# Seven-product block multiplication for seven of 22 up-projection pairs, three feed-forward blocks and edge copies on ScalarE, in a two-layer encoder step

## Chip, cores and metric

The kernel runs on one core of one Trainium2 chip. The metric is the device time of one execution in microseconds (us). TensorE (PE) does the matrix products, its weight loads are listed apart (PEld); VectorE (DVE), ScalarE (ACT) and GpSimd (POOL) do the element-wise work; SyncE (SP) issues the DMA transfers.

## The reference, cut to what matters

One inference step of a two-layer encoder for 544 columns of tokens (512 prompt, 32 sample), model width 1024, feed-forward width 2816, all in float32. The part that the change touches is the feed-forward of each layer:

```python
up = x @ lp['ffn_w_up']                                   # (544 x 1024) @ (1024 x 5632)
upc, ffn_conv_new = causal_dwconv(up, ffn_conv_prev, lp['ffn_conv_w'], lp['ffn_conv_b'])   # width 3
g_ff, val = upc[..., :D_FF], upc[..., D_FF:]
f = (jax.nn.gelu(g_ff) * val) @ lp['ffn_w_down']          # (544 x 2816) @ (2816 x 1024)
x = layer_norm(ALPHA * x + f, lp['ln2_g'], lp['ln2_b'])
```

`ffn_conv_new`, the last two rows of `up` of either group, is an output. Before the feed-forward stands the mixer (three head groups, an output projection and a layer norm).

## The kernel before, in words

**Layout.** Activations are kept transposed: a page is 128 features by 544 token columns, eight pages make the model width. Each float32 operand of a large product is split into a high part (a fp32r copy, on ACT) and a low part (source minus high, on DVE): `split` (L77). One k-tile of a product is three matmuls (`mm3`, L87: high x high on L88, high x low on L89, low x high on L90), each 128x128 weights by 272 columns, since a PSUM bank is filled for one half (`hv`) of the columns at a time.

**Feed-forward** (`ffn`, L1019). The 5632 up-projected features are 44 tiles of 128: 22 pairs, a gate tile (s = 0) and a value tile (s = 1). The work goes in two blocks (`NB`, L26) of 11 pairs. In a block, for each tile: `up_w` (L1008) loads 512 KB of weights through one of two raw buffers (`wr`) and splits them into one of five `wh` and one of five `wl` buffers; `mms` (L221) makes 8 k-tiles x 3 matmuls for each half; `ev` (L1031) evacuates: ACT copies the bank to `xp` (L1040) and makes the first convolution tap `ac` from the same bank (L1041). After the second half POOL copies the edge columns, the state in and the new state out (L1043 to L1045), DVE adds the other two taps (L1046, L1048), ACT applies the gelu to a gate tile (L1050), DVE multiplies the value tile with it (L1053), and the product is split into `fh`, `fl` (L1057). Then the block's down-projection runs over its 11 `fh`, `fl` pages: `proj` (L941) after the first block, `proj_ln` (L948) after the second. Both take the output tiles m = 0, 1 together (k-tile by k-tile in turn), then one by one; DVE adds each bank to the page `xT` (L1083, L1093).

**Start of the feed-forward.** While the last output-projection tiles are made, `proj_ln` prepares the weights of the first five up tiles (`pre_up`, L1011). The layer norm writes the pages XH, XL in the order m = 0..7: m = 0..3 before the last evacuations, m = 4..7 after them (L979, L985). `staged` (L1014) makes the first three up tiles together over the k-tiles m = 0..7 and then two tiles one by one; the second half's norm hangs as a hook behind the third k-tile. For the next eight tiles a `settle` (L935) finishes one page `xT` each (L1069).

**What sets the order.** Each engine runs its instructions in an order that is fixed when the program is built: of those that are ready, the one that stands first in the program. So a later piece of work can go ahead of an earlier one that waits, but only where the build foresaw the wait. PSUM has five banks for these products, eight `kb` pages hold `xp` and `ac`, and 28 `pg` and 12 `pt` pages hold the rest. The cache and state loads of the mixer have three raw pages of their own (`cr`).

Of the kernel before, what the change touches and what calls it, by code (L numbers as in the profile page):

```python
# [13 lines left out]
DEPTH = 2  # L14
# [8 lines left out]
PG = 552  # L23
D_FF = 2816
NI = 22
NB = 2  # L26
BI = NI // NB
# [18 lines left out]
def trunk_kernel(ctx: ExitStack, tc: tile.TileContext, i, o, k):  # L46
# [4 lines left out]
    BUFS = dict(pg=28, pt=12, kb=8, pp=6, cr=3, wr=2, wh=5, wl=5)  # L51

    def page(name, dt=F32, tag="pg"):
        return pool.tile([128, PG], dt, tag=tag, name=name, bufs=BUFS[tag])

# [31 lines left out]
    def mm3(ps, lh, ll, rh, rl, start, stop):  # L87
        nc.tensor.matmul(ps, lh, rh, start=start, stop=False)  # L88
        nc.tensor.matmul(ps, lh, rl, start=False, stop=False)  # L89
        lastmm[0] = nc.tensor.matmul(ps, ll, rh, start=False, stop=stop)  # L90

    gate = []
    def load_w(src, kk, cols, name):
        wr = pool.tile([128, kk, cols], F32, tag="wr", name=name + "r", bufs=BUFS["wr"])
        nc.sync.dma_start(out=wr, in_=src)
        return wr

# [135 lines left out]
    KX = [(XH[m], XL[m]) for m in range(8)]  # L233

# [474 lines left out]
    def cache_page(l, n):  # L709
        r = page("cr", tag="cr")  # L710
        nc.sync.dma_start(out=r[:, 0:512], in_=i["ck"][l, n])
        return r[:, 0:512].rearrange("p (t c) -> p t c", t=2)

    def sample_scores(l, ukT, csT):
# [3 lines left out]
        def keys(j):  # L718
            cT = []
            for c in range(2):  # L720
                raw = page("ckT", tag="cr")
# [4 lines left out]
            raw = page("krr", tag="cr")  # L726
# [54 lines left out]
    def sample_out(l, sp, csn):  # L781
# [30 lines left out]
        uvr = [page(f"uvs{c}", tag="cr") for c in range(2)]  # L812
# [201 lines left out]
    def staged(ws, hv, hook):  # L1014
        yield from enumerate(mms(ws[0:3], KX, hv, hook))
        for j in range(3, len(ws)):
            yield j, mms([ws[j]], KX, hv)[0]

    def ffn(l, va, vf, xT, first, hook, rest, pre):  # L1019
        fo = const([128, 176], F32, "fo")  # L1020
        fov = fo.rearrange("p (s j r) -> p s j r", s=2, j=2)

# [3 lines left out]
        for bl in range(NB):  # L1026
            fts = []
            tiles = [(BI * bl + j, s) for j in range(BI) for s in range(2)]
            xp, ac = {}, {}

            def ev(tl, hv, ps):  # L1031
                i_, s = tl
                r = NI * s + i_
                if hv == 0:
                    tag = "pg" if bl == 0 and tiles.index(tl) in (3, 4) else "kb"
                    xp[tl] = page("xp", tag=tag)
                    ac[tl] = page("ac", tag=tag)
                    nc.gpsimd.memset(xp[tl][:, 0:2], 0.0)  # L1038
                x, a = xp[tl], ac[tl]
                act(x[:, 2 + HW * hv:2 + HW * hv + HW], ps)  # L1040
                act(a[:, HV[hv]], ps, AF.Identity, scale=vfc(F_W + 88, r), bias=vfc(F_B, r))  # L1041
                if hv == 1:
# [3 lines left out]
                    stt(a[:, 0:W], x[:, 0:W], vfc(F_W, r), a[:, 0:W], ALU.mult, ALU.add)  # L1046
                    nc.vector.tensor_copy(out=x[:, 512:513], in_=fov[:, 0, 0, r:r + 1])
                    stt(a[:, 0:W], x[:, 1:1 + W], vfc(F_W + 44, r), a[:, 0:W], ALU.mult, ALU.add)  # L1048
                    if s == 0:
                        act(a[:, 0:W], a[:, 0:W], AF.Gelu_apprx_tanh)  # L1050
                    else:
                        g = ac.pop((i_, 0))
                        tt(a[:, 0:W], a[:, 0:W], g[:, 0:W], ALU.mult)  # L1053
                        j = i_ - BI * bl
                        tag = "pt" if (j < 6) == (bl == 0) and (bl == 0 or j >= 5) else "pg"
                        fh, fl = page("fh", F32R, tag), page("fl", F32R, tag)
                        split(fh[:, 0:W], fl[:, 0:W], a[:, 0:W])  # L1057
                        fts.append((fh, fl))
                        ac.pop(tl)
                    xp.pop(tl)  # L1060

            done = 0
            if bl == 0:
                done = len(first)
                for hv in range(2):
                    for j, ps in staged(first, hv, hook if hv == 0 else None):
                        ev(tiles[j], hv, ps)
            for tl in tiles[done:]:
                if rest:  # L1069
                    rest.pop(0)()  # L1070
                w = up_w(l, *tl)
                for hv in range(2):
                    ev(tl, hv, mms([w], KX, hv)[0])
            wd = i["wdn"][l, bl]

            def wsrc(m):
                return wd[m]

            if bl < NB - 1:
# [6 lines left out]
                proj(wsrc, fts, ev2, "wd", 6)  # L1086
            else:
# [6 lines left out]
                nxt = proj_ln(wsrc, fts, ln, "wd", 6, 2, pre, mid)  # L1094
# [26 lines left out]
def _layout(a):  # L1121
# [23 lines left out]
    d["wup"] = units(a["ffn_w_up"], 8)  # L1145
    w = a["ffn_w_down"].reshape(DEPTH, NB, BI, 128, 8, 128)
    d["wdn"] = w.transpose(0, 1, 4, 3, 2, 5).reshape(DEPTH, NB, 8, 128, BI * 128)
# [84 lines left out]
```

## Time and profile before

| what | value |
|---|---|
| median of 3 runs (lowest to highest) | 1288.82 us (1288.14 to 1291.58) |
| the profiled execution: its time | 1291.58 us |
| the profiled execution: its span | 1289.8 us, 24483 instructions |
| mean granted TensorE clock | 0.992 |

The profile is that of the slowest of the three executions. Busy time is per engine; a chain view follows the work that ended last, a wait view says which engine stood idle until what. Matmuls are pipelined, so the duration of one (some 288 ns) is longer than the step from one to the next. Times in the timeline are microseconds from the start of the span.

### The profile page before, as it was taken

To read this page: it belongs to the slowest core of one execution; us is meant where nothing else is said; L and a number is where in the kernel's file an instruction comes from. 1 tells how busy PE (TensorE), PEld (TensorE's weight loads), DVE (VectorE), ACT (ScalarE), POOL (GpSimd) and SP (SyncE) were. 2 spreads that over 40 slices of the span, in tenths; PEclk is the share of its full clock that TensorE was granted. 3 is DMA by queue.
4 is the path that set the end of the run, shared out by engine and by line. 5 is a ranking of instruction groups with operands and counts; after the bars stand their busy time and mean duration, and the time that the engine had idled before them with its cause. 6 is when DMAs were issued, how large, how long until landed. Compare 5 with 4: busy or idle time off the path is not lost.

```text
span 1289.8 us, 24483 instructions
## 1 busy us (share of the span) xinstructions
PE 1266.2 (98%) x9682; PEld 1224.4 (95%) x9682; DVE 835.4 (65%) x1695; ACT 674.4 (52%) x1357; POOL 140.7 (11%) x486
## 2 busy tenths in 40 slices
PE   8999999999999999999999999999999999999995
PEld 8999869899999999999999997899999999999995
DVE  5766866986653355654886868688765435556466
ACT  6575754485542255542475767547655314555332
POOL 2510000021210012210000100000221001121000
PEclk9999989999999999999999999999999999999998
DMA  8333322232213322223344432331322233222222
GB/s 271 116 111 117 107 85 92 66 101 96 74 57 100 117 97 83 81 71 101 93 138 141 120 98 72 101 110 52 100 82 71 72 104 108 90 83 78 61 79 70
DMA packets 51475, 124.63 MB, mean 97 GB/s; under 512 B 7832, under 2 KB 15512, under 8 KB 51360
## 3 DMA queue, kind: packets, MB, share of 16 engines
q1 hardware_dynamic: 51360, 123.06, 30.2%
q8 instruction: 76, 1.25, 0.4%
q14 instruction: 39, 0.32, 0.1%
HBM read 112.61 MB, written 5.97 MB: 92 GB/s over the span
## 4 chain that ended last, share of the span: by engine, by line
PE 91%; DVE 5%; DMA 2%; ACT 1%; issue 0%; DVEq 0%; ACTq 0%; SPq 0%
PE mm L89 25%; PE mm L88 25%; PE mm L90 25%; PE ov L239 2%; DVE xT L69 1%; PE pT L129 1%; PE ol L239 1%; DVE xT L66 1%; PE s L88 1%; PE s L89 1%; PE kv L384 1%; PE kv L383 1%; PE kv L385 1%; PE s L90 1%; DVE lnq L66 1%; DVE wupl L66 1%
## 5 line engine op out<-in xcount | busy, mean ns | idle before, releaser
L88 PE MATMUL mm<-xh,wuph 128*128 128x272 f32 x1408 | 404.0, 288 | 4.0 <-ACT xh L63 4.0
L89 PE MATMUL mm<-xl,wuph 128*128 128x272 f32 x1408 | 406.2, 289 | 0.1
L90 PE MATMUL mm<-xh,wupl 128*128 128x272 f32 x1408 | 405.7, 288 | 0.0
L88 PEld LDWEIGHTS mm<-xh,wuph 128*128 128x128 f32 x1408 | 264.3, 188 | 4.9 <-ACT xh L63 4.9
L89 PEld LDWEIGHTS mm<-xl,wuph 128*128 128x128 f32 x1408 | 265.1, 188 | 0.6 <-DVE xl L69 0.5
L90 PEld LDWEIGHTS mm<-xh,wupl 128*128 128x128 f32 x1408 | 264.7, 188 | 0.1
L66 DVE TENSOR_TENSOR wupl<-wupr,wuph 128x1024 fp32r<-128x1024 f32 (+1 forms) x94 | 108.8, 1157 | 107.4 <-ACT wuph L63 107.1
L69 DVE SCALAR_TENSOR_TENSOR ac<-xp,vf,ac 128x544 f32<-128x544 f32 x176 | 137.6, 784 | 30.3 <-POOL xp L1038 24.2
L1043 POOL COPY fo<-xp 128x2 f32<-128x2 f32 x88 | 73.1, 831 | 558.6 <-ACT xp L63 558.6
L63 ACT ACTIVATE wuph<-wupr 128x1024 fp32r<-128x1024 f32 (+1 forms) x94 | 94.3, 1005 | 65.9 <-PE mm L89 60.4
L63 ACT ACTIVATE xp<-mm 128x272 f32<-128x272 f32 x176 | 68.9, 391 | 106.2 <-PE mm L90 106.2
L63 ACT ACTIVATE ac<-mm,vf 128x272 f32<-128x272 f32 x176 | 101.3, 575 | 0.0
L63 ACT ACTIVATE fh<-ac 128x544 fp32r<-128x544 f32 x44 | 29.1, 661 | 59.2 <-DVE ac L66 59.2
L69 DVE SCALAR_TENSOR_TENSOR xT<-xT,mm 128x272 f32<-128x272 f32 x48 | 20.6, 438 | 52.1 <-PE mm L90 51.9
L66 DVE TENSOR_TENSOR fl<-ac,fh 128x544 fp32r<-128x544 f32 x44 | 31.9, 726 | 31.7 <-ACT fh L63 31.5
L582 DVE TENSOR_REDUCE sma<-s 128x1 f32<-128x128 f32 (+1 forms) x64 | 29.9, 486 | 17.3 <-PE s L90 16.7
L1038 POOL MEMSET xp<- 128x2 f32 x88 | 8.4, 97 | 286.6 <-PE gs L239 159.3
L63 ACT ACTIVATE ac<-ac 128x544 f32<-128x544 f32 x44 | 29.0, 660 | 20.2 <-DVE ac L69 20.1
L63 ACT ACTIVATE p<-s,sma 128x128 f32<-128x128 f32 (+1 forms) x64 | 33.4, 528 | 11.1 <-DVE sma L582 9.8
L63 ACT ACTIVATE lnt<-xT 128x272 f32<-128x272 f32 x56 | 22.6, 427 | 27.3 <-DVE xT L66 27.0
L66 DVE TENSOR_TENSOR ac<-ac 128x544 f32<-128x544 f32 x44 | 31.9, 725 | 1.4
L66 DVE TENSOR_TENSOR xT<-xT,mm 128x272 f32<-128x272 f32 x48 | 20.1, 439 | 18.7 <-PE mm L90 18.7
(490 smaller groups left out, 3461.3 us busy)
## 6 DMA issues: line engine op xcount, KB each, us to landing
wupr<-in_wup_dram SPq DMA_DIRECT2D x88, 512.0 KB
xT<-in_x_dram SPq DMA_DIRECT2D x16, 136.0 KB
xT<-in_x_dram SPq DMA_DIRECT2D x8, 272.0 KB
xd<-xT SPq DMA_DIRECT2D x8, 272.0 KB
xT<-xd SPq DMA_DIRECT2D x8, 272.0 KB
out_dram<-xT SPq DMA_DIRECT2D x16, 136.0 KB
ckT<-in_ckT_dram SPq DMA_DIRECT2D x8, 256.0 KB
cr<-in_ck_dram SPq DMA_DIRECT2D x8, 256.0 KB
```

The lines of the kernel that those rows point to most:

```text
L63: return nc.scalar.activation(out=out, in_=in_, func=func, **kw)
L66: return (e or nc.vector).tensor_tensor(out=out, in0=a, in1=b, op=op)
L69: return nc.vector.scalar_tensor_tensor(out=out, in0=a, scalar=s, in1=b, op0=op0, op1=op1)
L88: nc.tensor.matmul(ps, lh, rh, start=start, stop=False)
L89: nc.tensor.matmul(ps, lh, rl, start=False, stop=False)
L90: lastmm[0] = nc.tensor.matmul(ps, ll, rh, start=False, stop=stop)
L129: nc.tensor.transpose(out, in_, ident[0:p, 0:p])
L239: nc.tensor.matmul(ps, a, b, start=start, stop=stop)
L383: nc.tensor.matmul(b[0:n, 0:288], XH[j][:, cs], wh[:, ci, :], start=j == 0, stop=False)
L384: nc.tensor.matmul(b[0:n, 0:288], XL[j][:, cs], wh[:, ci, :], start=False, stop=False)
L582: nc.vector.tensor_reduce(out=sm[:, 0:1], in_=b[:, 0:n], axis=AX.X, op=ALU.max, negate=True)
L1043: nc.gpsimd.tensor_copy(out=fov[:, 0, :, r], in_=x[:, 512:514])
```

## The change

- Seven pairs of each layer (`SPL`: 8, 10, ..., 20) are made by a block multiplication with seven products instead of eight. The 2x2 blocks are: gate tile and value tile, the two halves of the model width, the two halves of the columns. `forms` makes the seven weight blocks (A11, A12, A22 and four sums) from the two raw weight tiles and splits them: three splits of 128x1024 and one of 128x512, and four DVE sums of 128x512. `mixed_x` makes four sums of the token halves for each pair of pages, once per layer, and splits them; they stay in 16 pages. A `product` is 4 k-tiles x 3 matmuls. `seven` orders the seven products in three parts; between the parts (`yield`) stand the halves of the gate tile of the next, ordinary pair. Products are summed partly in PSUM and partly by ACT and DVE.
- The feed-forward runs in three blocks of 7, 7 and 8 pairs (`BLK`).
- The k-tiles of the up-projection are taken in the order m = 0, 2, 4, 6, 1, 3, 5, 7 (`KO`), and the weights are laid out so.
- The edge copies move from POOL to ACT, two instructions for a tile; the first tap of a seven-product tile is made from `xp` in SBUF over 544 columns.
- The raw weight buffers go from two to four, and the three `cr` pages are dropped: cache and state loads use raw weight buffers too. A page is 550 wide instead of 552, `pp` pages 544. Down-projection weights come in one piece per tile and block.

```diff
-PG = 552
+PG = 550
-NB = 2
-BI = NI // NB
+BLK = ((0, 7), (7, 7), (14, 8))
+SPL = (8, 10, 12, 14, 16, 18, 20)
+KO = (0, 2, 4, 6, 1, 3, 5, 7)
-    BUFS = dict(pg=28, pt=12, kb=8, pp=6, cr=3, wr=2, wh=5, wl=5)
+    BUFS = dict(pg=28, pt=12, kb=8, pp=6, wr=4, wh=5, wl=5)
+    KU = [KX[m] for m in KO]
...
-        yield from enumerate(mms(ws[0:3], KX, hv, hook))
+        yield from enumerate(mms(ws[0:3], KU, hv, hook))
...
+    def forms(l, i_):
+        w = [load_w(i["wup"][l, NI * s + i_].rearrange("p (k c) -> p k c", k=8), 8, 128, "wup") for s in range(2)]
+        (a11, a12), (a21, a22) = [(r[:, 0:4, :], r[:, 4:8, :]) for r in w]
...
+        fa, fb, fc, fd = pair(8), pair(8), pair(8), pair(4)
+        split(*fa, w[0])
+        split(*fd, a22)
+        tt(a22, a21, a22, ALU.add)
+        tt(a21, a11, a21, ALU.subtract)
+        tt(a11, a22, a11, ALU.subtract)
+        tt(a12, a12, a11, ALU.subtract)
+        split(*fb, w[1])
+        split(*fc, w[0])
+        return dict(A11=(fa, 0), A12=(fa, 4), A22=(fd, 0), S3=(fb, 0), S1=(fb, 4), S2=(fc, 0), S4=(fc, 4))
+
+    def product(b, form, rhs, start=False):
+        (wh, wl), c = form
+        for k in range(4):
+            mm3(b[:, 0:HW], wh[:, c + k, :], wl[:, c + k, :], *rhs[k], start and k == 0, k == 3, skip_group_check=not start)
+
+    def mixed_x(xT, q):
+        x0, x1 = xT[2 * q], xT[2 * q + 1]
...
+        tt(t1, x0[:, h1], x0[:, h0], ALU.subtract)
+        tt(t3, x1[:, h1], x0[:, h1], ALU.subtract)
+        tt(t2, x1[:, h1], t1, ALU.subtract)
+        tt(t4, x1[:, h0], t2, ALU.subtract)
+        r = []
+        for raw in (ra, rb):
+            th, tl = page("th", F32R), page("tl", F32R)
+            split(th[:, 0:W], tl[:, 0:W], raw[:, 0:W])
...
+        def settle():
+            if rest:
+                rest.pop(0)()
+                if len(rest) % 2 == 0:
+                    TX.append(mixed_x(xT, len(TX)))
...
-                    nc.gpsimd.tensor_copy(out=fov[:, 0, :, r], in_=x[:, 512:514])
-                    nc.gpsimd.tensor_copy(out=x[:, 512:514], in_=vf[:, F_ST + r:F_ST + r + 45:44])
-                    nc.gpsimd.tensor_copy(out=fov[:, 1, :, r], in_=x[:, 544:546])
+                act(fov[:, :, :, r], x[:, 482:546].rearrange("p (s c) -> p s c", s=2)[:, :, 30:32])
+                act(x[:, 512:514], vf[:, F_ST + r:F_ST + r + 45:44])
...
-                        tag = "pt" if (j < 6) == (bl == 0) and (bl == 0 or j >= 5) else "pg"
+                    tag = "pt" if i_ - i0 < 6 else "pg"
...
+            def seven(i_):
...
+                b1, b2 = bank("mm"), bank("mm")
+                product(b1, f["A11"], x[0], start=True)
+                product(b2, f["A12"], x[1], start=True)
+                begin(g)
+                c11 = half(g, 0)
+                act(c11, b2[:, 0:HW])
+                tt(c11, c11, b1[:, 0:HW], ALU.add)
+                yield
+                product(b1, f["S2"], t[2])
+                u2 = page("u2", tag="pp")[:, 0:HW]
+                act(u2, b1[:, 0:HW])
+                b5 = bank("mm")
+                product(b5, f["S1"], t[0], start=True)
+                product(b1, f["S3"], t[1])
+                begin(v)
+                c22 = half(v, 1)
+                act(c22, b5[:, 0:HW])
+                tt(c22, c22, b1[:, 0:HW], ALU.add)
+                yield
+                product(b5, f["S4"], x[2])
+                tt(half(g, 1), u2, b5[:, 0:HW], ALU.add)
+                first_tap(g, ac[g][:, 0:W], xp[g][:, 2:2 + W])
+                post(g)
+                product(b1, f["A22"], t[3])
+                act(half(v, 0), b1[:, 0:HW])
+                first_tap(v, ac[v][:, 0:W], xp[v][:, 2:2 + W])
+                post(v)
...
             for tl in tiles[done:]:
-                if rest:
-                    rest.pop(0)()
+                settle()
+                if tl[0] in SPL:
+                    if tl[1] == 0:
+                        mix = seven(tl[0])
+                        next(mix)
+                    continue
                 w = up_w(l, *tl)
                 for hv in range(2):
-                    ev(tl, hv, mms([w], KX, hv)[0])
+                    ev(tl, hv, mms([w], KU, hv)[0])
+                    if mix is not None and next(mix, True):
+                        mix = None
...
-                return wd[m]
+                return i["wdn"][l, m, :, 128 * i0:128 * (i0 + nk)]
...
-                proj(wsrc, fts, ev2, "wd", 6)
+                proj(wsrc, fts, ev2, "wd", 8)
...
-                nxt = proj_ln(wsrc, fts, ln, "wd", 6, 2, pre, mid)
+                nxt = proj_ln(wsrc, fts, ln, "wd", 8, 2, pre, mid)
```

`raw_page` (new) takes a page of 512 columns from the raw weight buffers; `cache_page`, the key loads and the value-weight loads of the mixer use it in place of `cr`. `post` is the part of `ev` that followed the second half.

## Rows read from the trace of the kernel before

**Rows 1.** The page: busy time of each engine and its share of the span

```profile
PE 1266.2 (98%) x9682; PEld 1224.4 (95%) x9682; DVE 835.4 (65%) x1695; ACT 674.4 (52%) x1357; POOL 140.7 (11%) x486
```

**Rows 2.** Waits of PE: who for whom, total us, times, longest us

```profile
PE mm L88 <- ACT xh L63: 8.5, 4, 4.1
PE ln L886 <- DVE lns L66: 0.6, 1, 0.6
```

**Rows 3.** Busy time by stretch: us, engines, clock, DMA share, GB/s

```profile
375.70:442.00 66.30, 66.30 (x532) 66.30 (x531) 24.67 (x36) 15.18 (x20) 0.97 (x4) 1.00 0.31 95
442.00:575.00 133.00, 133.00 (x1062) 133.00 (x1061) 77.06 (x107) 71.59 (x130) 24.60 (x83) 1.00 0.26 85
```

**Rows 4.** PE timeline (start us, us): second block's first up, first down matmul

```profile
441.85 0.28 PE L88 MATMUL mm<-xh,wuph 128*128 128x272 f32 x1
...
574.43 0.29 PE L88 MATMUL mm<-fh,wd0h 128*128 128x272 f32 x1
```

**Rows 5.** DVE instruction groups by shape: busy us, mean ns, idle before, releasers

```profile
L69 DVE SCALAR_TENSOR_TENSOR ac<-xp,vf,ac 128x544 f32<-128x544 f32 x176 | 137.6, 784 | 30.3 <-POOL xp L1038 24.2 <-POOL xp L1044 2.0 <-ACT ac L63 1.3
L66 DVE TENSOR_TENSOR wupl<-wupr,wuph 128x1024 fp32r<-128x1024 f32 x82 | 100.5, 1226 | 107.3 <-ACT wuph L63 107.1
L66 DVE TENSOR_TENSOR fl<-ac,fh 128x544 fp32r<-128x544 f32 x44 | 31.9, 726 | 31.7 <-ACT fh L63 31.5
L66 DVE TENSOR_TENSOR ac<-ac 128x544 f32<-128x544 f32 x44 | 31.9, 725 | 1.4
L66 DVE TENSOR_TENSOR xT<-xT,mm 128x272 f32<-128x272 f32 x48 | 20.1, 439 | 18.7 <-PE mm L90 18.7
L1047 DVE COPY xp<-fo 128x1 f32<-128x1 f32 x88 | 13.3, 153 | 2.7
L66 DVE TENSOR_TENSOR wupl<-wupr,wuph 128x512 fp32r<-128x512 f32 x12 | 8.3, 692 | 0.1
```

**Rows 6.** ACT instruction groups by shape, same columns

```profile
L63 ACT ACTIVATE ac<-mm,vf 128x272 f32<-128x272 f32 x176 | 101.3, 575 | 0.0
L63 ACT ACTIVATE wuph<-wupr 128x1024 fp32r<-128x1024 f32 x82 | 87.0, 1061 | 62.1 <-PE mm L89 60.4
L63 ACT ACTIVATE xp<-mm 128x272 f32<-128x272 f32 x176 | 68.9, 391 | 106.2 <-PE mm L90 106.2
L63 ACT ACTIVATE fh<-ac 128x544 fp32r<-128x544 f32 x44 | 29.1, 661 | 59.2 <-DVE ac L66 59.2
L63 ACT ACTIVATE xT<-xT,va 128x544 f32<-128x544 f32 x24 | 16.8, 749 | 0.0
L63 ACT ACTIVATE wuph<-wupr 128x512 fp32r<-128x512 f32 x12 | 7.3, 623 | 3.8 <-DMA wupr<-in_wup_dram 3.8
L63 ACT ACTIVATE xh<-so 64x32 fp32r<-64x32 f32 x16 | 3.1, 191 | 7.6 <-DVE xl L66 7.6
```

**Rows 7.** PE timeline at the start of the first feed-forward

```profile
241.48 0.65 PE L88 MATMUL mm<-xh,wuph 128*128 128x272 f32 x3 [2.05 <-ACT xh L63]
...
248.15 0.64 PE L88 MATMUL mm<-xh,wuph 128*128 128x272 f32 x3
```

**Rows 8.** ACT timeline, same place

```profile
247.58 1.34 ACT L63 ACTIVATE xh<-xT,va 128x272 fp32r<-128x272 f32 x3
```

**Rows 9.** ACT timeline, end of the second block's up-projection

```profile
574.50 0.85 ACT L63 ACTIVATE wd2h<-wd2r 128x768 fp32r<-128x768 f32 x1 [1.09 <-PE mm L89]
575.25 0.38 ACT L63 ACTIVATE xp<-mm 128x272 f32<-128x272 f32 x1
...
579.31 0.66 ACT L63 ACTIVATE fh<-ac 128x544 fp32r<-128x544 f32 x1 [3.21 <-DVE ac L66]
```

**Rows 10.** DVE timeline, same place

```profile
580.01 0.73 DVE L66 TENSOR_TENSOR fl<-ac,fh 128x544 fp32r<-128x544 f32 x1 [0.79 <-ACT fh L63]
```

**Rows 11.** DVE timeline, two independent instructions in a row

```profile
388.97 0.83 DVE L66 TENSOR_TENSOR wd2l<-wd2r,wd2h 128x640 fp32r<-128x640 f32 x1 [4.35 <-ACT wd2h L63]
389.71 0.95 DVE L66 TENSOR_TENSOR wd3l<-wd3r,wd3h 128x768 fp32r<-128x768 f32 x1
```

More of the change, by code (lines that the diff above doesn't have):

```diff
@@ L85, in vsplit, with mm3 @@
         tt(lo, src, hi.bitcast(F32), ALU.subtract)
[L87 to L90, printed above, removed]
+    def mm3(ps, lh, ll, rh, rl, start, stop, **kw):
+        nc.tensor.matmul(ps, lh, rh, start=start, stop=False, **kw)
+        nc.tensor.matmul(ps, lh, rl, start=False, stop=False, **kw)
+        lastmm[0] = nc.tensor.matmul(ps, ll, rh, start=False, stop=stop, **kw)
     gate = []
@@ L720, in keys @@
             for c in range(2):
-                raw = page("ckT", tag="cr")
+                raw = raw_page("ckT")
                 nc.sync.dma_start(out=raw[:, 0:512], in_=i["ckT"][l, j, c])
@@ L725, in keys @@
                 cT.append((ch, cl))
-            raw = page("krr", tag="cr")
+            raw = raw_page("krr")
             nc.sync.dma_start(out=raw[0:96, 0:512], in_=i["krT"][l][:, 512 * j:512 * j + 512])
@@ L811, in sample_out @@
         yield
-        uvr = [page(f"uvs{c}", tag="cr") for c in range(2)]
+        uvr = [raw_page(f"uvs{c}") for c in range(2)]
         for c in range(2):
@@ L1029, in ffn, with begin, half, first_tap @@
             xp, ac = {}, {}
-            def ev(tl, hv, ps):
+            def begin(tl):
+                tag = "pg" if bl == 0 and tiles.index(tl) in (3, 4) else "kb"
+                xp[tl] = page("xp", tag=tag)
+                ac[tl] = page("ac", tag=tag)
+                nc.gpsimd.memset(xp[tl][:, 0:2], 0.0)
+            def half(tl, hv):
+                return xp[tl][:, 2 + HW * hv:2 + HW * hv + HW]
+            def first_tap(tl, out, src):
+                r = NI * tl[1] + tl[0]
+                act(out, src, AF.Identity, scale=vfc(F_W + 88, r), bias=vfc(F_B, r))
@@ L1032, in ev, with post @@
+            def ev(tl, hv, ps):
+                if hv == 0:
+                    begin(tl)
+                act(half(tl, hv), ps)
+                first_tap(tl, ac[tl][:, HV[hv]], ps)
+                if hv == 1:
+                    post(tl)
+            def post(tl):
                 i_, s = tl
                 r = NI * s + i_
[L1034 to L1038, printed above, removed]
@@ new lines, in seven @@
+            def seven(i_):
+                g, v = (i_, 0), (i_, 1)
+                f = forms(l, i_)
+                x = [[(p[0][:, c], p[1][:, c]) for p in KU[4 * h:4 * h + 4]] for h, c in ((0, HV[0]), (1, HV[0]), (1, HV[1]))]
+                t = list(zip(*TX))
+                b1, b2 = bank("mm"), bank("mm")
[25 more added lines that the diff above has]
+                post(v)
```

64 lines of the change are left out of this document (34 added, 30 removed).

## The prediction, made before the changed kernel ran

> **What bounds the kernel now.** I read the busy shares first: PE works 98% of the span, DVE 65%, ACT 52% [rows 1]. A busy PE need not be a PE without gaps, so the waits of PE came next: of four entries over the whole span the longest are 8.5 and 0.6 us, both at layer-norm seams; none is for a load, none lies inside a feed-forward block [rows 2]. The windows by stretch show the same: in an up-projection block and in a down-projection PE is busy all the time at the full granted clock (1.00, that is 2.4 GHz), while DVE has 77.1 us of work in 133.0 us and ACT 71.6 [rows 3]. So in the feed-forward the time is the number of matmuls times their step. The step comes from the timeline: the second block's up-projection begins at 441.85 and its down-projection at 574.43 us [rows 4]; 132.58 us for 22 tiles x 48 = 1056 matmuls is 0.1256 us each.
>
> **What the change removes.** An ordinary pair costs 2 tiles x 2 halves x 8 k-tiles x 3 = 96 matmuls, a seven-product pair 7 x 4 x 3 = 84. Over 14 pairs that is 168 matmuls fewer: 168 x 0.1256 = 21.1 us. The down-projection keeps its matmuls (7 + 7 + 8 = 22 k-tiles). The Trainium skill (TensorE: Matmul & The Clock Gate, Back-to-back issue gap) gives columns / 2.4 + 2.5 ns for a warm matmul, 116 ns for 272 columns, 9 ns below the measured step; by it the term would be 19.5 us. No other term uses that figure.
>
> **What it adds, and what covers it.**
>
> *DVE and ACT work.* An ordinary pair costs DVE two weight splits (1.226 us), four taps (0.784), two small copies (0.153), the product and the split of `fh` (0.725, 0.726): 7.35 us [rows 5]. A seven-product pair replaces the two splits by three and one of half size (0.692), adds four sums of 128x512 (I take 0.692 each) and three sums out of PSUM (0.439, the nearest row): +1.23 + 0.69 + 2.77 + 1.32 = +6.0, so 13.4 us. On ACT an ordinary pair has two splits (1.061), four copies (0.391), four first taps (0.575), a gelu and a split (0.661 each): 7.3 us. The other pair adds 1.061 + 0.623 and makes the four taps as two of 544 columns (0.749): 8.2 us [rows 6]. Each of the four tiles gets two edge copies; the nearest row is a 64x32 copy, 0.191, so +1.5 us. One ordinary and one seven-product pair alternate: 180 matmuls = 22.6 us of PE, 20.7 us of DVE (92%), 17.0 of ACT (75%). Both fit, DVE barely. Instructions that don't depend on each other overlap: one of 0.83 us is followed 0.74 us later [rows 11], which eases it by some 5%. `mixed_x` is 4 x (4 x 0.439 + 2 x 0.726) = 12.8 us of DVE and 5.3 of ACT in the first block of each layer, whose PE time after the first tiles is some 60 us; the third block's 16 extra evacuations are 7.0 us of DVE in down-projections where it has 24.7 us of work in 66.3 [rows 3]. All at nothing as long as PE's next weights lie ready; if the cover is gone, the DVE rival below prices it. The third block adds no matmul.
>
> *Places where PE now waits for a result.* In each seven-product pair a bank that PE goes on adding to must be read first. Between S2 and S3 stand 12 matmuls, 1.5 us; the read needs the last matmul's tail (0.29), a copy (0.39) and a signal, 0.75 us, and up to 1.06 more where ACT has just begun a weight split: 0.3 us late at worst. Before S2 stand 24 matmuls, 3.0 us, against 0.3 + 0.4 + 0.44 + signals, 1.3 us, and at worst 1.06 + 1.23 more: 0.6 late. With as much again for weights that come late (four of the five `wh`, `wl` buffers belong to one seven-product pair), a pair loses 0 to 1.2 us. Such an engine has a long instruction in hand about a quarter of the time: I take 0.25, 14 x 0.25 = **3.5 us** (0 to 17).
>
> *The k order.* At the start of a feed-forward PE begins at 241.48 with the first three tiles and gets m = 4 at 248.15 [rows 7], because ACT makes xh of m = 4 only at 247.58 [rows 8]. Between lie 41 matmuls, nearly all of m = 0..3. In the new order the third k-tile is m = 4 and the fourth m = 6, so before it only m = 0 and 2 can run: 18 matmuls for the three tiles, 30 with the two single tiles drawn forward (that PE's order is shifted so is seen in row 7: three L88 in a row). 11 to 23 matmuls, 1.4 to 2.9 us, are lost per layer. I take 1.6, as the two banks for those should be free by then: **3.2 us** (0 to 5.8).
>
> *Six seams from up to down instead of four, with shorter cover.* After the down-projection's start at 574.43 the last pair's `fh` is ready at 579.31 + 0.66 = 579.97 and `fl` at 580.74 [rows 9, 10], 6.3 us later; the last of 11 k-tiles is due after 60 matmuls, 7.5 us. With 7 k-tiles it is due after 36 (4.5 us), with 8 after 42 (5.3 us): `fl` is 1.7 and 0.9 us late. The edge copies on ACT shorten the chain: POOL ended 0.3 us after ACT (DVE idled 24.2 us over 74 taps for it [rows 5]). That leaves 1.4 and 0.6: 4 x 1.4 + 2 x 0.6 = 6.8 us if PE stands still, nothing if the second half's matmuls, which need two free banks, are put ahead. I take 0.3 a seam: **1.8 us** (0 to 6.8).
>
> *The rest at nothing.* POOL's copies leave an engine that is 11% busy. Mixer loads share four raw buffers with weights instead of 2 + 3: PE waits there for no load now [rows 2], so it can lose but little; I take 0, between -1 and +2.
>
> **Sum.** -21.1 + 3.5 + 3.2 + 1.8 = -12.6 us, against the profiled execution's own 1291.58 us (span 1289.8): 1279.0. That execution was 2.8 us above the median of 1288.82, so for the median I give **1276 us**. A measurement of this kernel can tell about 0.3%, 3.9 us, from no change.
>
> **Rivals.**
>
> *DVE becomes the bound (slower).* With 20.7 of 22.6 us DVE may idle 1.9 us in a cycle of two pairs before PE stands still, and 3.4 us before the gain is gone (24.1 us for two ordinary pairs). Against it: of DVE's present idle time most is waiting for ACT's high part (107.1 us before `wupl`, 31.5 before `fl`), which other work could fill. For it: where it isn't filled, three `forms` splits behind 1.06 us, one behind 0.62 and two `fl` behind 0.8 make 5.4 us, the cycle 26.1, 2.0 over the present: 14 x 2.0 + 5.0 for the seams and the k order is +33, 1322 us; half that idling (2.7) gives 23.4 a cycle and with the upper ends of the seams 1289 to 1295. I put this case at 1293 to 1322, chance 0.11. The Trainium skill (VectorE: DVE Perf Modes, The DRAIN you can't avoid) says that the next instruction doesn't start until the pipe is empty; by that nothing of the 92% would be eased. Row 11 speaks against it.
>
> *All waits are filled (full gain).* The order of each engine is laid at build time, and PE's gaps inside the blocks are zero now. If the three costs vanish: 1288.8 - 21.1 = 1267.7 us; 1267 to 1270. For it, the mechanism seen in row 7; against it, the k order has nothing more to draw forward. Chance 0.17.
>
> *The gain is eaten (no change).* The k order at 5.8, the seams at 6.8 and 0.6 us a pair make 21.0 us: 1288.7. That takes each wait at its upper half. Chance 0.11.
>
> That it doesn't do what it says can only be that the matmul count doesn't fall by 168; by the diff it must, so no chance goes there.
>
> **How the numbers follow.** Forecast (gain of 6 to 17 us, 1271 to 1283) 0.61, full gain 0.17, no change 0.11, slower 0.11. Faster by over 0.3% are the first two: 0.78; same 0.11; slower 0.11. The range leaves out the slower case and part of the two neighbours: 1267 to 1288.
>
> **What would show it.** PE x9514 in the page, 168 fewer, at the same step. In the windows of the second and third block PE should be busy nearly all the time with DVE at 85 to 92%; PE waits on DVE or ACT below `product` of a few tenths each, in sum under 5 us. At the start of either feed-forward, a PE gap (or slow steps) of 1 to 3 us before m = 4. At the six seams, second-half matmuls ahead of the last k-tile, or a PE wait for `fl`. POOL near 31 us (140.7 less its three copies). The forecast is wrong if PE stands still by over 1 us in most seven-product pairs, if the mixer's stretch changes by more than 2 us, or if the granted clock drops in the blocks.

## The result, and the profile after

The changed kernel takes **1273.1 us** (1272.04 to 1275.62), beside 1290.08 us for the kernel before in the same comparison (four executions, one more than in the table above): ratio **0.9872** with an interval of 0.985 to 0.9894, 17 us or 1.3% faster. The prediction was 1276 us, with 1267 to 1288 as its range. The sign and the size came out as forecast; what the gain is made of did not, so that the near hit is partly luck, and the experiments are about that.

The profiled execution took 1273.21 us, its span is 1271.2 us. The page's busy times, the answer to [rows 1]:

```profile
PE 1247.2 (98%) x9514; PEld 1202.8 (95%) x9514; DVE 920.4 (72%) x1885; ACT 710.3 (56%) x1533; POOL 48.4 (4%) x222
```

x9514 is the forecast count, 168 matmuls fewer. The waits of PE, the answer to [rows 2] (who waits for whom, total us, times, longest us):

```profile
PE mm L89 <- ACT xh L64: 5.7, 2, 4.1
PE ln L891 <- DVE lns L67: 2.4, 2, 1.8
PE mm L89 <- DVE xT L67: 0.9, 2, 0.4
PE mm L89 <- ACT fh L64: 0.4, 2, 0.2
```

Nothing in the list lies inside a seven-product pair. Two waits are new in size: 1.6 us for `xh` behind the 4.1 us at the very start, and 1.8 us for `lns`; both stand at the end of a feed-forward. The timeline of PE there, in the first layer (start us, us, and in brackets the idle time before it):

```profile
628.13 0.29 PE L91 MATMUL mm<-fh,wd7l 128*128 128x272 f32 x1
630.03 0.39 PE L89 MATMUL mm<-xh,win0h 128*128 128x272 f32 x1 [1.62 <-ACT xh L64]
```

Before, the same place had a wait of 0.36 us. The windows, the answer to [rows 3] (window, its length, then busy us of PE, PEld, DVE, ACT, POOL, the granted clock, DMA share, GB/s): the first down-projection, the up-projections of the second and third block, and, from one C11 sum to the next, one cycle of an ordinary and a seven-product pair:

```profile
320.20:362.80 42.60, 42.40 (x339) 42.18 (x338) 20.82 (x32) 9.23 (x13) 0.20 (x2) 1.00 0.23 75
362.80:443.40 80.60, 80.60 (x638) 79.97 (x637) 56.65 (x87) 50.17 (x106) 1.10 (x11) 1.00 0.32 98
486.10:577.70 91.60, 91.60 (x722) 90.64 (x721) 68.21 (x106) 58.01 (x122) 1.88 (x16) 1.00 0.33 101
...
515.54:538.58 23.04, 23.04 (x182) 22.72 (x181) 18.63 (x31) 15.11 (x33) 0.40 (x4) 1.00 0.29 92
```

The second block has 14 x 48 less 3 x 12 = 636 matmuls; at 0.12555 us they make 79.85 us, and the stage lasts 80.64 (from its first matmul at 362.79 to the first of the down-projection at 443.43). The third has 720, 90.40 us, and lasts 91.64 (486.08 to 577.72). So a seven-product pair loses 0.79 / 3 = 0.26 and 1.24 / 4 = 0.31 us. In the third block the loss stands at two places of each pair but the first: the first two steps of S2, right behind the C11 sum, are 0.16 us too long together, and the first two of S3, behind the copy `u2` that frees its bank, 0.25 us. DVE is busy 18.63 of 23.04 us in a cycle (81%).

DVE groups, the answer to [rows 5] (busy us, mean ns, idle before and its releasers):

```profile
L70 DVE SCALAR_TENSOR_TENSOR ac<-xp,vf,ac 128x544 f32<-128x544 f32 x176 | 134.3, 779 | 1.7
L67 DVE TENSOR_TENSOR wfwl<-wupr,wfwh 128x1024 fp32r<-128x1024 f32 x42 | 51.3, 1221 | 19.7 <-ACT wfwh L64 19.7
L67 DVE TENSOR_TENSOR wupr<-wupr 128x512 f32<-128x512 f32 x56 | 38.5, 687 | 0.7
```

The sums of forms cost 0.687 us each, as taken (0.692). The taps' idle time fell from 30.3 to 1.7 us: their wait for POOL is gone.

### The profile page after: what moved, and what is told of

The parts are those of the page before. It is cut to its first block, busy times and chain, and to the rows that moved or that the text cites. A ratio compares the mean times of both kernels' runs of the same rounds, so it can differ in the third digit from the quotient of the medians.

```text
span 1271.2 us, 24212 instructions
## 1 busy us (share of the span) xinstructions
PE 1247.2 (98%) x9514; PEld 1202.8 (95%) x9514; DVE 920.4 (72%) x1885; ACT 710.3 (56%) x1533; POOL 48.4 (4%) x222
## 4 chain that ended last, share of the span: by engine, by line
PE 87%; DVE 7%; ACT 3%; DMA 1%; issue 1%; DVEq 0%; ACTq 0%
PE mm L89 24%; PE mm L90 24%; PE mm L91 23%; DVE xT L70 2%; PE ov L244 1%; DVE ac L70 1%; PE pT L133 1%; PE ol L244 1%; PE s L89 1%; PE kv L389 1%; PE kv L390 1%; PE kv L388 1%; PE s L90 1%; PE s L91 1%; DVE xT L67 1%
## 5 line engine op out<-in xcount | busy, mean ns | idle before, releaser
L90 PE MATMUL mm<-xl,wuph 128*128 128x272 f32 x960 | 276.4, 288 | 0.0
L91 PE MATMUL mm<-xh,wupl 128*128 128x272 f32 x960 | 276.2, 288 | 0.0
L89 PE MATMUL mm<-xh,wuph 128*128 128x272 f32 x960 | 275.1, 289 | 0.9 <-DVE xT L67 0.9
L89 PEld LDWEIGHTS mm<-xh,wuph 128*128 128x128 f32 x960 | 180.1, 188 | 1.6 <-DVE xT L67 1.3
L90 PEld LDWEIGHTS mm<-xl,wuph 128*128 128x128 f32 x960 | 180.6, 188 | 0.2
L91 PEld LDWEIGHTS mm<-xh,wupl 128*128 128x128 f32 x960 | 180.6, 188 | 0.0
L67 DVE TENSOR_TENSOR wfwl<-wupr,wfwh 128x1024 fp32r<-128x1024 f32 (+1 forms) x56 | 61.0, 1089 | 32.2 <-ACT wfwh L64 31.8
L89 PE MATMUL mm<-th,wfwh 128*128 128x272 f32 x224 | 65.6, 297 | 0.0
L91 PE MATMUL mm<-th,wfwl 128*128 128x272 f32 x224 | 64.1, 288 | 0.0
L90 PE MATMUL mm<-tl,wfwh 128*128 128x272 f32 x224 | 64.1, 288 | 0.0
```

The lines of the kernel that those rows point to most:

```text
L67: return (e or nc.vector).tensor_tensor(out=out, in0=a, in1=b, op=op)
L89: nc.tensor.matmul(ps, lh, rh, start=start, stop=False, **kw)
L90: nc.tensor.matmul(ps, lh, rl, start=False, stop=False, **kw)
```

## The experiments

Ratios are against the kernel before on the same chip; differences between two kernels are taken from their ratios, times 1288 us. The kernel before against itself and the changed kernel again show what a comparison can tell.

**The kernel before, unchanged.**

> The kernel before, unchanged, to see whether the stretch at half clock in the first mixer (some 11 us at 0.5 to 0.6 of the clock, 165 to 176 us into the span) belongs to it. If it belongs to the kernel: the mean granted clock is 0.992 in each run, the span 1286 to 1290 us, and the first mixer's stretch from the first value-and-gate product to the first output-projection matmul is again some 92.6 us against 87.0 in the second layer. If it was chance in one profile: runs without it are some 4.6 us shorter, about 1285 us of span.

Measured: 1288.08 us, ratio 1.0005 (0.9996 to 1.0014). In this profile the granted clock is 1.00 from 165 to 176 us and the span 1286.4 us, so the stretch doesn't belong to the kernel.

**The changed kernel again:**

> The changed kernel, unchanged, on the chip of the three kernels beside it: 0.987 of before again (0.985 to 0.989).

Measured: 1272.33 us, 0.9873 (0.9856 to 0.9891). So the ratio repeats; its interval is some 2 us to either side.

**Only the raw buffers.** The kernel before with nothing but the four shared raw buffers and the narrower pages:

```diff
-    BUFS = dict(pg=28, pt=12, kb=8, pp=6, cr=3, wr=2, wh=5, wl=5)
+    BUFS = dict(pg=28, pt=12, kb=8, pp=6, wr=4, wh=5, wl=5)
-        r = page("cr", tag="cr")
+        r = raw_page("cr")
...
```

> The kernel before with the raw buffers of the change alone (four shared ones instead of two and three, narrower pages). Theory 1, that the gain outside the feed-forward comes from the raw buffers: the start of the feed-forward comes some 3 us earlier in the first layer and 1.5 in the second, the PE gap of 2.0 us ahead of the first up matmul goes, time 4 to 9 us below before (ratio 0.993 to 0.997). Theory 2, that it comes from the other order of work: same as before within 1 us (0.999 to 1.001).

Measured: 1279.38 us, ratio **0.9936** (0.9923 to 0.995). Half of the whole gain, 8.2 us, comes from a part that I had put at nothing. PE's longest waits in this kernel:

```profile
PE mm L88 <- ACT xh L63: 4.1, 1, 4.1
PE pT L132 <- ACT pt L63: 0.3, 2, 0.2
```

Of [rows 2] only the wait at the very start is left, 8.5 + 0.6 us became 4.1 plus trifles. The 2.05 us ahead of the first up matmul [rows 7] are gone in both layers. What changed ahead of it is seen in the group of the splits of the first five up tiles on ACT, between 200 and 245 us of the kernel before (count, min, median and max ns, first and last start us) and who kept ACT idle:

```profile
L63 ACT ACTIVATE wuph<-wupr x8: 614/632/1063, 212.6 to 234.5; 128x512 fp32r<-128x512 f32 x6, 128x1024 fp32r<-128x1024 f32 x2
...
  DMA wupr<-in_wup_dram: 2.3, 3
```

and the same group with four raw buffers, between 195 and 240 us:

```profile
L63 ACT ACTIVATE wuph<-wupr x8: 614/632/1048, 205.1 to 216.1; 128x512 fp32r<-128x512 f32 x6, 128x1024 fp32r<-128x1024 f32 x2
```

With two raw buffers the last splits stood 7 us ahead of the first up matmul, among the `lnt` squares of the layer norm, and ACT waited there for their DMA; with four they are over 19.4 us ahead of it (216.1 and 235.54). The norm's chain has ACT for itself. ACT's waits for these weights did not go: they are 3.9 us in this window (2.3 before), but they come earlier, and PE waits for nothing there. What shows is the 2.05 us twice and the 0.96 of the two other waits that went (0.36 and 0.6), 5.1 us of 8.2; the first up-projection is 0.7 us a layer shorter besides (from its first matmul to that of the down-projection 133.56 and 133.57 us, before 134.24 and 134.20), and the rest wasn't taken apart. The run changes the number of buffers, their sharing and the page width at once, and with them the order that the build lays; which of these does it stays open.

**No seven-product pair.** The changed kernel with every pair ordinary, all else kept:

```diff
-SPL = (8, 10, 12, 14, 16, 18, 20)
+SPL = ()
-                if len(rest) % 2 == 0:
-                    TX.append(mixed_x(xT, len(TX)))
```

> The changed kernel with an empty list of seven-product pairs and without the mixed token pages: all 22 pairs ordinary, three blocks, edges on ScalarE, four raw buffers. It shows the seven-product part by itself as the difference to the changed kernel. If that part gives its 168 matmuls less 0.3 us a pair: 21.1 - 4 = 17 us more than the changed kernel, that is about 1290 us, no gain over before. If the surroundings bring 9 us by themselves and cost 5 in the seams: about 1286 (ratio 0.996 to 0.998).

Measured: 1290.63 us, ratio **1.0017** (1.0005 to 1.0029). With the runs above the gain comes apart: buffers 0.9936, then three blocks with edge copies on ScalarE and the new k order 1.0017 (+10.4 us), then the seven products 0.9872 (**-18.7 us**). The stages of the profiles give a smaller number for the last step. The windows of this kernel's second and third block, and of the start of its second mixer:

```profile
364.28:448.57 84.29, 84.29 (x674) 84.29 (x673) 47.58 (x66) 48.80 (x107) 1.30 (x13) 1.00 0.26 82
491.17:587.49 96.32, 96.32 (x770) 96.32 (x769) 55.09 (x76) 56.62 (x123) 1.66 (x16) 1.00 0.27 88
...
640.00:645.00 5.00, 4.96 (x28) 4.74 (x27) 4.99 (x14) 3.50 (x7) 0.00 (x0) 0.66 0.00 0
```

The changed kernel needs 80.64 and 91.64 us for these two blocks, in the second layer 80.81 and 91.69 (here again 84.29 and 96.32): the seven products bring **16.4 us**, and 4.7 of the 21.1 us of matmuls are lost, 0.33 us a pair. What the times have beyond that lies outside these stages: the profile of this kernel has stretches at the lower clock near 167 and 642 us that the changed kernel's doesn't have. The last row shows the second one (0.66 on average), right behind a wait of 1.63 us. The mean granted clocks of the eleven executions, 0.992 to 0.997, broadly fall as their times rise from 1287.57 to 1294.18 us.

The +10.4 us can be read in the same way. From the kernel with four raw buffers to this one the profiles differ by 11.0 us: 4.2 in the two feed-forwards, 1.8 and 1.9 behind their last matmuls, 3.1 in the second mixer, where the stretch above lies.

**The old k order.** The first five up tiles take m = 0..7 in turn again:

```diff
-        yield from enumerate(mms(ws[0:3], KU, hv, hook))
+        ws = [[w[KO.index(m)] for m in range(8)] for w in ws]
+        yield from enumerate(mms(ws[0:3], KX, hv, hook))
...
```

> The changed kernel with the first five up tiles taken in the old order of k-tiles m = 0..7 (the weights indexed to fit). My prediction of 1.6 us a layer for the new order: 3 us faster than the changed kernel, about 1270 us. The trace, in which the start of the feed-forward loses as much time as before: no difference, 1273 us within 1 us.

Measured: 1270.76 us, 0.987 (0.9856 to 0.9883); in the time it can't be told from the changed kernel. In the trace it can, by the first block's up-projection. PE's first up and first down matmul of the changed kernel:

```profile
234.03 0.54 PE L89 MATMUL mm<-xh,wuph 128*128 128x272 f32 x3
...
320.21 0.29 PE L89 MATMUL mm<-fh,wd0h 128*128 128x272 f32 x1
```

and with the old order:

```profile
235.08 0.29 PE L89 MATMUL mm<-xh,wuph 128*128 128x272 f32 x1
...
320.40 0.29 PE L89 MATMUL mm<-fh,wd0h 128*128 128x272 f32 x1
```

86.18 against 85.32 us: the new order costs **0.86 us a layer**. The two kernels below that differ in the same way show 86.17 and 85.30.

**Three tiles in turn at the feed-forward's end.** The first halves of the last three instead of two output tiles are made ahead of the second halves:

```diff
-                nxt = proj_ln(wsrc, fts, ln, "wd", 8, 2, pre, mid)
+                nxt = proj_ln(wsrc, fts, ln, "wd", 8, 3, pre, mid)
```

> The changed kernel with three instead of two output tiles held back at the end of the last down-projection (24 more matmuls, 3.0 us, behind the first half's layer-norm sums). Theory: with blocks of 8 instead of 11 k-tiles only 6 + 24 = 30 matmuls (3.8 us) are left behind those sums, where before it was 15 + 33 = 48 (6.0 us), and PE waits 1.6 us before the second layer's first product and 1.8 us before the last sums. Then the waits go: 2.5 to 3.4 us faster than the changed kernel, and no PE wait over 0.5 us at either place. Rival: the layer norm's chain on DVE and ACT has the same length from the last evacuation and the wait only moves: same within 1 us.

Measured: **1268.07 us** (1266.82 to 1268.4), ratio **0.9838** (0.9821 to 0.9854): 4.4 us faster than the changed kernel. The layer norm's statistics hang behind the sixth k-tile of the first second-half tile. With 11 k-tiles 5 x 3 + 33 = 48 matmuls stood behind it, 6.0 us; with 8 there are 2 x 3 + 24 = 30, 3.8 us; a third tile makes 54. PE's waits now:

```profile
PE mm L89 <- ACT xh L64: 4.1, 1, 4.1
PE mm L89 <- DVE xT L67: 0.9, 2, 0.5
```

Both seam waits are gone.

**Both mends together**, the old k order and three tiles:

```diff
...
+        yield from enumerate(mms(ws[0:3], KX, hv, hook))
...
+                nxt = proj_ln(wsrc, fts, ln, "wd", 8, 3, pre, mid)
```

> The changed kernel with both mends together: three output tiles in turn at the end of the second layer's and first layer's last down-projection, and the first five up tiles in the old k order. If they add: 1268.1 less 0 to 2 us, 1266 to 1268 us. If the old k order is worth nothing, 1268 us; a time above 1270 would say that they disturb each other.

Measured: 1267.79 us, 0.9844 (0.9829 to 0.9859). They don't disturb each other, and the 1.7 us of the k order is below what the times can tell. This and the one above are the fastest kernels of the study; both beat the changed kernel.

**The edge copies back on GpSimd**, three a tile as before:

```diff
-                act(fov[:, :, :, r], x[:, 482:546].rearrange("p (s c) -> p s c", s=2)[:, :, 30:32])
-                act(x[:, 512:514], vf[:, F_ST + r:F_ST + r + 45:44])
+                nc.gpsimd.tensor_copy(out=fov[:, 0, :, r], in_=x[:, 512:514])
+                nc.gpsimd.tensor_copy(out=x[:, 512:514], in_=vf[:, F_ST + r:F_ST + r + 45:44])
+                nc.gpsimd.tensor_copy(out=fov[:, 1, :, r], in_=x[:, 544:546])
```

> The changed kernel with the edge copies back on GpSimd (three a tile). My step: the copies on ScalarE shorten the chain at the six seams by 0.3 us each, and nothing else; so at most 2 us slower with them on GpSimd. Rival: ScalarE, freed of 176 copies of some 0.2 us (35 us), evacuates earlier in the seven-product pairs: up to 3 us faster.

Measured: 1289.16 us, ratio **1.0002** (0.9991 to 1.0013). All of the gain is gone with the two ScalarE instructions a tile; I had expected 2 us at most. PE's waits:

```profile
PE mm L89 <- ACT wuph L64: 7.2, 10, 0.7
PE mm L89 <- ACT fh L64: 5.7, 6, 1.3
```

The 5.7 us are the six seams. The 7.2 us are in the cycles, where the weights of the ordinary tile come late. How, is seen in one of them, first on POOL:

```profile
516.25 0.32 POOL L1107 COPY fo<-xp 128x2 f32<-128x2 f32 x1 [2.52 <-ACT xp L64]
516.51 1.20 POOL L1109 COPY fo<-xp 128x2 f32<-128x2 f32 x1
517.65 0.69 POOL L1108 COPY xp<-vf 128x2 f32<-128x2 f32 x1
```

Three copies of two columns take 2.1 us, and the first tap waits for the last of them. On ACT, same place:

```profile
514.85 1.06 ACT L64 ACTIVATE wfwh<-wupr 128x1024 fp32r<-128x1024 f32 x1 [0.64 <-DVE wupr L67]
515.81 0.38 ACT L64 ACTIVATE xp<-mm 128x272 f32<-128x272 f32 x1
516.09 0.57 ACT L64 ACTIVATE ac<-mm,vf 128x272 f32<-128x272 f32 x1
516.56 0.66 ACT L64 ACTIVATE fh<-ac 128x544 fp32r<-128x544 f32 x1
517.13 1.99 ACT L64 ACTIVATE wuph<-wupr 128x1024 fp32r<-128x1024 f32 x2
```

ACT waits for one of DVE's sums of forms, which in this kernel stands behind two taps in DVE's order (in the changed kernel ahead of them); the split of `wuph` follows late, and PE, due at 517.4, gets it at 518.22. The order of instructions is not that of the changed kernel: it is laid at build time, and it moved with the copies. On DVE one of the two splits `wupl` of the ordinary tiles now stands behind the C11 sum, which starts at 520.28:

```profile
521.32 1.22 DVE L67 TENSOR_TENSOR wupl<-wupr,wuph 128x1024 fp32r<-128x1024 f32 x1
```

In the changed kernel both stand ahead of it. What that costs is worked out with the doubled splits below.

**One edge copy on GpSimd**, the one for which no tap waits:

```diff
-                act(fov[:, :, :, r], x[:, 482:546].rearrange("p (s c) -> p s c", s=2)[:, :, 30:32])
+                act(fov[:, 0, :, r], x[:, 512:514])
                 act(x[:, 512:514], vf[:, F_ST + r:F_ST + r + 45:44])
+                nc.gpsimd.tensor_copy(out=fov[:, 1, :, r], in_=x[:, 544:546])
```

> The changed kernel with one of a tile's edge copies on GpSimd: that of the sample part's new state, for which no tap waits. The copy of the prompt part's new state and the old state's copy into the page, for which the first DVE tap waits, stay on ScalarE. Theory A (what cost 16.8 us was GpSimd in the chain from the second half's copy to the first tap): 0 to 3 us slower than the changed kernel, 1272 to 1276 us. Theory B (work on GpSimd as such, or the order that the build lays once a third engine takes part, is the cost): over 6 us slower, 1279 to 1290.

Measured: 1273.55 us, 0.9885 (0.9865 to 0.9905), as the changed kernel, with 88 copies more on POOL. So POOL may work; what costs is POOL in the chain from the bank to the tap, by its time and by the order that the build lays for it, which the runs don't part.

**GpSimd copies without seven-product pairs**, two of the edits above in one kernel:

```diff
-SPL = (8, 10, 12, 14, 16, 18, 20)
+SPL = ()
...
+                nc.gpsimd.tensor_copy(out=fov[:, 0, :, r], in_=x[:, 512:514])
+                nc.gpsimd.tensor_copy(out=x[:, 512:514], in_=vf[:, F_ST + r:F_ST + r + 45:44])
+                nc.gpsimd.tensor_copy(out=fov[:, 1, :, r], in_=x[:, 544:546])
```

> No seven-product pair, three blocks, and the three edge copies a tile back on GpSimd. Theory A (the copies on ScalarE are worth 17 us only because DVE's order has no room in a seven-product cycle; in ordinary pairs the GpSimd chain is hidden and costs only at the seams to the down-projections): 0 to 5 us slower than without seven-product pairs and with ScalarE copies (1290.6), so 1290 to 1296 us. Theory B (three blocks or the copies as such make GpSimd's chain costly): 12 to 17 us slower, 1303 to 1308.

Measured: 1292.99 us, ratio 1.0043 (1.0026 to 1.006): 3.3 us slower than without them, not 16.6. PE's wait that stands for it is that of the seams alone (0.8 us with the ScalarE copies):

```profile
PE mm L89 <- ACT fh L64: 3.1, 6, 0.5
```

In ordinary pairs the chain is hidden. The two parts of the change need each other: the seven products leave the tap's chain no room.

**More work for DVE in the weights' chain.** Two of a pair's low parts are computed twice, in `forms` (2 x 1.22 us a pair):

```diff
         split(*fc, w[0])
+        for (hi, lo), src in ((fb, w[1]), (fc, w[0])):
+            tt(lo, src, hi.bitcast(F32), ALU.subtract)
```

> The changed kernel with two of the four low parts of each seven-product pair computed twice (the same values again): 2 x 1.23 = 2.45 us more on VectorE for each such pair, 34 us in all, nothing else. My reading that VectorE has 92% of its cycle filled and some 5% of that overlapped: 19.7 + 2.45 = 22.1 of 22.6 us, PE stands still by less than 0.5 us a pair, 0 to 7 us slower. Rival, that VectorE is the bound already: each added us is paid in full, 34 us slower. Rival, that it has much slack: no change within 1 us.

Measured: 1301.55 us, ratio 1.0101 (1.0081 to 1.0121): 29.2 us slower for 34 us of work. My own reading had 0 to 7 us. That looks like a DVE that is full. PE's waits, and the window of one cycle (it ends 0.2 us short of the next C11 sum, at 547.99):

```profile
PE mm L89 <- DVE xp L67: 20.1, 10, 2.1
```

```profile
521.49:547.78 26.29, 24.39 (x180) 24.17 (x180) 20.51 (x32) 14.95 (x32) 0.40 (x4) 0.94 0.22 79
```

But DVE is busy only 20.51 of 26.29 us, and the timeline of DVE shows where it idles, right behind the sum that PE had waited for (C11 at 521.49, C22 at 529.65):

```profile
521.49 0.43 DVE L67 TENSOR_TENSOR xp<-xp,mm 128x272 f32<-128x272 f32 x1
521.84 0.71 DVE L67 TENSOR_TENSOR ac<-ac 128x544 f32<-128x544 f32 x1
522.48 1.21 DVE L67 TENSOR_TENSOR wupl<-wupr,wuph 128x1024 fp32r<-128x1024 f32 x1
523.61 0.71 DVE L67 TENSOR_TENSOR fl<-ac,fh 128x544 fp32r<-128x544 f32 x1
524.25 1.21 DVE L67 TENSOR_TENSOR wupl<-wupr,wuph 128x1024 fp32r<-128x1024 f32 x1
529.65 0.44 DVE L67 TENSOR_TENSOR xp<-xp,mm 128x272 f32<-128x272 f32 x1 [4.19 <-PE mm L91]
```

**As much work for DVE in its gap.** Six subtractions of 128x272, which nobody reads, directly behind the C11 sum:

```diff
                 tt(c11, c11, b1[:, 0:HW], ALU.add)
+                dm = page("dm", tag="pp")
+                for _ in range(6):
+                    tt(dm[:, 0:HW], c11, c11, ALU.subtract)
                 yield
```

> The changed kernel with six additional DVE subtractions of 128x272 a seven-product pair, whose result nobody reads, directly behind the first sum of C11 (84 in all; each follows the one before after about 0.35 us in the rows of this kernel, so 2.1 us a pair, 29 us in all: nearly what the doubled splits added). Theory A (DVE is no bound by its amount of work; PE waits only for work that stands in DVE's order between the C22 sum and the next C11 sum, and behind C11 DVE idles 2.8 us in each cycle): 0 to 4 us slower than the changed kernel, 1272 to 1277 us, and no PE wait of over 0.5 us for xp. Theory B (DVE's sum of work is the bound, so each us is paid wherever it stands): 20 to 29 us slower, 1292 to 1302 us.

Measured: 1272.57 us, ratio 0.9884 (0.9867 to 0.99), the same as the changed kernel, with 84 instructions more (36.9 us by the group's busy time). One cycle's window, and DVE's timeline from C11 to C22:

```profile
516.46:539.50 23.04, 23.04 (x182) 22.72 (x181) 21.01 (x37) 15.11 (x33) 0.40 (x4) 1.00 0.28 94
```

```profile
516.46 0.43 DVE L67 TENSOR_TENSOR xp<-xp,mm 128x272 f32<-128x272 f32 x1
516.81 0.71 DVE L67 TENSOR_TENSOR ac<-ac 128x544 f32<-128x544 f32 x1
517.44 0.91 DVE L67 TENSOR_TENSOR dm<-xp 128x272 f32<-128x272 f32 x2
518.27 0.72 DVE L67 TENSOR_TENSOR fl<-ac,fh 128x544 fp32r<-128x544 f32 x1
518.90 1.86 DVE L67 TENSOR_TENSOR dm<-xp 128x272 f32<-128x272 f32 x4
521.07 0.44 DVE L67 TENSOR_TENSOR xp<-xp,mm 128x272 f32<-128x272 f32 x1 [0.30 <-PE mm L91]
```

DVE is busy 21.01 of 23.04 us here, 91%, and nothing is lost; with 20.51 us of work in the window of the other kernel ten cycles were longer, six by 2.2 us and four, in which the clock fell, by 3.5. So DVE's amount of work is not the bound. What the rows show is a loop through the orders of DVE and PE:

- PE starts S2, and S3 behind it, only after the C11 sum, which reads the same bank. In the changed kernel this sum ends at 515.97 and S2 begins at 516.03: there is no room. (S1 has a bank of its own; the build put it ahead of S2.)
- The C22 sum needs S3. From C11 to C22 it takes 4.6 us, in which DVE idles 2.8.
- Behind C22 DVE has the next pair's forms, the taps and the other splits, and then the next C11: 18.4 us with 1.6 us of gaps (520.15 to 538.54).

With the doubled splits C22 to C11 still takes 18.3 us, since the build put two splits of `wupl`, 1.2 us each, behind C11 (at 522.48 and 524.25 in the rows above). But 22 matmuls of an ordinary tile then had to go from ahead of S2, where PE now waits, to between S2 and S3 (524.74 to 527.75), and C11 to C22 grew from 4.6 to 6.9 us in six cycles and to 8.15 in the four. 20.1 of the 29.2 us are listed waits, the rest is mostly slow matmuls behind them. The kernel with the copies on GpSimd shows the same: with one `wupl` split behind C11 it has 7.1 us from C11 to C22 and 17.0 from C22 to C11, 24.1 us a cycle in place of 23.0. No run changes the order alone, so that the order costs it is read from these rows and not from a run of its own.

## Why the prediction was right, and where it was not

The time came within 4 us of the forecast partly by luck: a gain of 8.2 us and an added cost of 5.4 us, neither of them foreseen, partly cancel. In three steps of one chain, by the ratios:

| part | predicted | measured |
|---|---|---|
| raw buffers, narrower pages | 0 (-1 to +2) | -8.2 |
| k order, seams, third block, edge copies | +3.2 + 1.8 = +5.0 | +10.4 |
| seven products | -21.1 + 3.5 = -17.6 | -18.7 |
| sum | -12.6 | -16.5 |

The parts hold for this order of steps only: with the edge copies on GpSimd the seven products bring 5 us (1.0043 to 1.0002), not 18.7. By stages of the profiles the second row is 4.2 us in the feed-forwards and 3.7 at their ends, the third -16.4; with the -8.2 they make -16.7.

**Matmuls and product waits: right.** 168 fewer at the same step, and 0.33 us a pair lost by the stages (0.17 by the times, whose intervals are wider than this difference) where 0.25 was taken. There is no listed wait inside `product`; what is lost are single steps at the two places that were named, S2 and S3. One reading was wrong: I had S1's 12 matmuls between S2 and S3. The build put S1 ahead, and only four matmuls stand between the last of S2 and the first of S3. (And 116 ns is 10 ns below the step of 125.6, not 9.)

**The rest at nothing: wrong for the buffers.** I wrote that PE waits there for no load now, so it can lose but little, and looked only for a loss. The sign that I named for a wrong forecast, a mixer stretch that changes by more than 2 us, came: from the kernel before run again to the changed kernel run again the first mixer (up to the first up matmul) goes from 236.62 to 233.57 us, the second from 230.28 to 228.05. PE waited for `xh` [rows 7], and ACT, on the way to it, for a DMA: the row is in [rows 6], 3.8 us before `wuph` of 128x512, released by `wupr`. Such a row next to a PE wait makes a gain possible; by itself it says little, since in the changed kernel the same row has 8.8 us and PE's wait is gone: it matters where in ACT's order it stands. With the wait at the 2.05 us of [rows 7] in two layers and 0.96 of the two others I would have had -5.

**The k order: half its price.** 1.6 us a layer taken, 0.86 measured. The expected gap is there, 0.44 us of PE waiting for `xT` at 237.79, not the 1 to 3 us named; `xh` of m = 4 comes 5.7 us after the start (239.71 and 234.03), not 6.1.

**The seams: those from up to down at twice the price, the two at the end missed.** I took 0.3 us for each of six from up to down. The two in the middle of the first layer lose 0.50 and 0.57 us (the first down-projection lasts 362.79 - 320.21 = 42.58 us, 336 matmuls at 0.12525 make 42.08), 0.20 of it as a wait for `fh`; those of the second layer lose 0.51 and 0.88. But I looked only at the side of the down-projection where its k-tiles start. The same shorter run of k-tiles also covers the layer norm at its other end, and there 3.8 us in place of 6.0 made waits of 1.62 and 1.76 us, and 4.4 us in all as the mend shows. k order 1.7, middle seams 2.5 and end seams 4.4 make 8.6 of the 10.4 us. The rest is covered by the second mixer of the kernel without seven-product pairs, with its stretch at the lower clock: 230.64 us in its profile, 227.50 with four raw buffers and 228.05 in the changed kernel run again. So some 2 us stand in the 10.4 and in the 18.7 with opposite signs and are not of the change.

**The edge copies: their worth was not seen.** They stood in the sum as a cost of 1.5 us of ACT and as some tenths at a seam. Without them the change gains nothing. The hint was in [rows 5]: 24.2 us of DVE idling for POOL. I used it for 0.3 us at a seam, and didn't ask what becomes of it once DVE's cycle has to fit.

**The DVE rival: it did not come, for a reason that I had only partly.** I summed DVE's cycle as 20.7 of 22.6 us. In the trace it is 18.63 of 23.04, as instructions that follow each other overlap by 0.07 to 0.09 us each; 31 of them make the 2 us (I had taken 5%). The window of 85 to 92% that I named was therefore not there (70% and 74% in the blocks). What the rival had wrong is the sum over the cycle: 2.45 us more in the chain of the weights cost 29.2 of 34 us, as much in the gap behind C11 cost nothing. (The case with half the idling adds up to 1291.6 us at most, 1288.8 - 9.8 + 12.6, not to the 1295 given there.) On the rule that I weighed there, the Trainium skill (VectorE: DVE Perf Modes, The DRAIN you can't avoid): the prediction used half of it. The section also says that an instruction which is not held starts earlier, and for independent instructions these traces agree with that (0.43 us followed after 0.35). The subtractions that write the same page don't overlap: two last 0.91 us, four 1.86, 0.46 each, a little more than one alone.

**POOL** came to 48.4 us, not near 31: the 110 us were a sum of durations. The three copies' durations make 109.4 us, but they overlap, and their busy time was 98.7 of the 140.7 us [rows 1]; the other work took 48.4 in place of 42.0.

## What to carry to other kernels

An engine that works in a fixed order can be bound by a loop and not by its share, as here: follow one result from the engine to PE and back to the same engine, and sum what stands between in both orders. When the number of k-tiles of a product changes, look at both ends of it for what it covers. A DMA wait that stands on the engine right ahead of a PE wait is worth pricing as a gain, even where the change mentions the buffers only in passing.

## What the runs showed of the hardware

A standstill of PE can cost more than its length. In the kernel with the doubled splits PE waited ten times 1.85 to 2.11 us; after four of these the next 15 or 16 matmuls came at 0.23 in place of 0.126 us each, 1.5 us more in sum (0.4 after the other six). The windows of this kernel before and after one such wait (1.91 us, to 521.98; the granted clock is the third number from the end):

```profile
518.00:519.70 1.70, 1.70 (x16) 1.70 (x15) 1.70 (x4) 1.68 (x3) 0.10 (x1) 1.00 0.91 301
...
523.00:524.00 1.00, 1.00 (x6) 1.00 (x6) 1.00 (x2) 0.25 (x1) 0.00 (x0) 0.50 0.00 0
...
526.00:528.00 2.00, 2.00 (x18) 2.00 (x17) 0.00 (x0) 0.00 (x0) 0.00 (x0) 1.00 0.72 248
```

0.50 is the 1.2 GHz level, 1.00 the 2.4 GHz level. After the other six waits, of the same lengths, the clock stayed at 1.00, as it did after the 1.62 us in the changed kernel. After the same wait (1.61 to 1.63 us) it fell to 0.50 in three other kernels of the study: without seven-product pairs, with all copies on GpSimd, and with the six subtractions; in the kernel before run again it fell after one of 1.99 us. What decides is not seen in these runs. And a copy of two columns on GpSimd, 0.32 to 1.20 us in the rows above, takes ScalarE 0.20 us on the mean (88 of `xp<-vf`, 17.7 us).
